# One level of Strassen–Winograd for both feed-forward products of a decoder layer

## The chip, the cores and the metric

The kernel runs on one core of one Trainium2 chip. The metric is device time in microseconds (us) of one execution. Five engines work side by side, each through its own queue of instructions in order: TensorE (PE in the profile, with its weight loads as PEld), VectorE (DVE), ScalarE (ACT), GpSimd (POOL) and SyncE (SP), which here issues the DMAs. SBUF is the on-chip memory, PSUM holds the matmul results, DRAM is the memory beyond.

## What is computed

The reference is one layer of a hybrid decoder, then a final norm, for 1024 tokens, model width 1024 and a feed-forward width of 4096, all in float32:

```
u = RMSNorm(h);  z = u @ W_in
branches: sparse attention, a gated recurrence, cross attention into 256 memory tokens
h += W_o( sum_b sigmoid(gate_b(u)) * y_b )
h += W_down( relu(RMSNorm(h) @ W_up)^2 )      # W_up 1024 x 4096, W_down 4096 x 1024
out = RMSNorm(h)
```

Only the last two lines and W_o bear on this change.

## The kernel before

Every float32 product is done in three passes (`mm3`, L219): each operand is split into a high part (`hi`, rounded to the fast type fp32r) and the rest (`lo`), and hi·hi, hi·lo and lo·hi are added up in PSUM. `split` makes the two: the high part is a copy on ACT (L216), the low part a subtraction (L217) on DVE or, if the caller says so, on POOL. A scheduler orders the instructions of each engine after the program has been written, so the source shows what depends on what, and a listing of the built program shows the order.

W_o (`out_proj`, L1002 to L1036) goes by eight tiles of 128 tokens: load `yr`, split it, 48 matmuls, add the residual (L1021), normalise (`rms_scale`, L203), transpose eight blocks on PE (L84), and write the normalised activations, scaled by `gmlp`, as `vh` and `vl` with the feature in the partition (L1033, L1034).

The feed-forward part (L1066 to L1119) goes by 16 blocks of two chunks of 128 of the 4096 hidden features. For a chunk and a half of the tokens, 24 matmuls give 128 x 512 of the hidden layer in the PSUM tile `psg`; ACT takes relu (L1083) and its square (L1084, the high part), DVE the square in float32 (L1085) and the low part (L1086). Then, for eight token tiles and two halves of the width, 12 matmuls give the block's share of the down product in `pss` or `pst`, and DVE adds it to `h`, which stays in SBUF (L1107). The next block's weights are loaded meanwhile (`uraw` 512 KB, `draw` 256 KB, SP's queue) and split by ACT and POOL. After the last block each token tile is normalised (L1109 to L1118) and written out (L1119).

Of the kernel before, what the change touches and what calls it, by code (L numbers as in the profile page):

```python
# [9 lines left out]
F32 = mybir.dt.float32  # L10
# [56 lines left out]
class TensorQueue:  # L67
    """TensorE's instructions, with the sum of their cost."""
# [7 lines left out]
    def matmul(self, out, w, x, start, stop):  # L76
        n = 1
        for d in out.shape[1:]:
            n *= d
        self.tc.nc.tensor.matmul(out, w, x, start=start, stop=stop)  # L80
        self._add(n)
# [54 lines left out]
def body(tc, A, out):  # L136
# [4 lines left out]
    with ExitStack() as top:  # L141
# [3 lines left out]
        w4 = top.enter_context(tc.tile_pool(name="w4", bufs=1))  # L145
# [32 lines left out]
        tn_d = dram.tile([KC, P, S], F32, name="tn_d")  # L178
        y_d = [dram.tile([KC, P, 512], F32, name=f"y_d{x}") for x in range(2)]
# [39 lines left out]
        def mm3(ps, sh, sl, mh, ml, first, last):  # L219
            pe.matmul(ps, sh, mh, start=first, stop=False)  # L220
            pe.matmul(ps, sh, ml, start=False, stop=False)
            pe.matmul(ps, sl, mh, start=False, stop=last)
# [12 lines left out]
        with ExitStack() as mid:  # L235

# [68 lines left out]
            with tc.tile_pool(name="e0", bufs=1) as e0:  # L305
# [32 lines left out]
                def load_const(name, shape):  # L338
                    t = const.tile(shape, F32, name="c_" + name)
                    dma(t, A[name])  # L340
                    return t

                gmlp = load_const("g_mlp", [P, KC])
# [7 lines left out]
                wmask = const.tile([P, 640], BF16, name="wmask")  # L351
# [6 lines left out]
                gates = const.tile([P, NQ, 48], F32, name="gates")  # L358
                cp = const.tile([P, KC], F32, name="cp")
                cn = const.tile([P, KC], F32, name="cn")  # L360
                cn2 = const.tile([P, KC], F32, name="cn2")
                KCAB = const.tile([P, G, 2, 64], F32R, name="KCAB")
                VC = const.tile([64, G, P], F32R, name="VC")
# [630 lines left out]
            vp = mid.enter_context(tc.tile_pool(name="vp", bufs=1))  # L994

            def v_tiles(name):
                return [[vp.tile([P, 4, 512], F32R, name=f"{name}{a}{b}") for b in range(2)] for a in range(2)]

            h = []
            vh = v_tiles("vh")  # L1000
            vl = v_tiles("vl")

            def out_proj():
                for j in range(NQ):
                    ts = slice(j * P, (j + 1) * P)
                    yh = w4.tile([P, KC, P], F32R, name="yh", tag="whi", bufs=2)
                    yl = w4.tile([P, KC, P], F32R, name="yl", tag="wlo", bufs=2)
                    for x in range(2):
                        yr = half2("yr").rearrange("p (c t) -> p c t", t=P)
                        dma(yr, y_d[j // 4][4 * x:4 * x + 4, :, (j % 4) * P:(j % 4) * P + P].rearrange("c p t -> p c t"))  # L1010
                        split(yh[:, 4 * x:4 * x + 4, :], yl[:, 4 * x:4 * x + 4, :], yr)
                    xt = st("xres")
                    dma(xt, A["x"][ts, :])
                    h.append(rw("h") if j < 6 else w4.tile([P, D], F32, name="h", tag="wraw", bufs=2))
                    for nh in range(2):
                        cs = slice(nh * 512, nh * 512 + 512)
                        ps = ps_g()
                        for k in range(KC):
                            woh, wol = wo[2 * nh + k // 4]
                            mm3(ps, yh[:, k, :], yl[:, k, :], woh[:, k % 4, :], wol[:, k % 4, :], k == 0, k == KC - 1)  # L1020
                        dve.scalar_tensor_tensor(h[j][:, cs], ps, 0.5, xt[:, cs], OP.mult, OP.add)  # L1021
                    r = rms_scale(h[j], xt)
                    dve.tensor_scalar(xt, h[j], r, None, OP.mult)
                    dst = tok_dst(vh, vl, j)
                    for kh in range(2):
                        pt = ps_s()
                        for k in range(4):
                            c = (kh * 4 + k) * P
                            pe.transpose(pt[:, k * P:(k + 1) * P], xt[:, c:c + P], ident)
                        dh, dl = dst(kh)  # L1030
                        for k in range(4):
                            g = gmlp[:, kh * 4 + k:kh * 4 + k + 1]
                            act.activation(dh[:, k, :], pt[:, k * P:(k + 1) * P], AF.Copy, scale=g)  # L1033
                            dve.scalar_tensor_tensor(dl[:, k, :], pt[:, k * P:(k + 1) * P], g, dh[:, k, :],  # L1034
                                                     OP.mult, OP.subtract)
                    yield  # L1036

            for _ in out_proj():
                pass

            def pair(name):
                t = big.tile([P, 2, S], F32R, name=name, tag="ut", bufs=8)
                return t[:, 0, :], t[:, 1, :]

            acts = [pair("act") for _ in range(4)]
            wds = [pair("wd") for _ in range(4)]
            NB = 2
            NBLK = FF // P // NB

            def load_up(fc):  # L1050
                raw = st("uraw", F32, (P, KC, P))
                dma(raw, A["w_up"][fc])
                wh = w4.tile([P, KC, P], F32R, name="uh2", tag="whi", bufs=2)
                wl = w4.tile([P, KC, P], F32R, name="ul2", tag="wlo", bufs=2)
                split(wh, wl, raw, lo_eng=pool)
                return wh, wl

            def load_down(fc):
                d_h, d_l = wds[fc % 4]
                for x in range(2):  # L1060
                    cs = slice(x * 512, x * 512 + 512)
                    raw = half2("draw")
                    dma(raw, A["w_down"][fc * P:(fc + 1) * P, cs])
                    split(d_h[:, cs], d_l[:, cs], raw, lo_eng=pool)

            up = [load_up(f) for f in range(NB)]  # L1066
            for f in range(NB):
                load_down(f)
            for fb in range(NBLK):
                fcs = [fb * NB + f for f in range(NB)]  # L1070
                order = [(f, hf) for f in range(NB) for hf in range(2)]
                if fb == 0:
                    order = [(f, hf) for hf in range(2) for f in range(NB)]
# [158 lines left out]
```

## Time and profile before

| what | value |
|---|---|
| runs | 2231.94 us median of 3 (2228.72 to 2233.19) |
| the profiled execution, first to last instruction | 2226.8 us |
| mean granted TensorE clock in it (1 is full speed) | 0.980 |
| PE busy | 94% of the span |
| DVE, ACT, POOL busy | 60%, 48%, 24% of the span |
| DMA | 191.20 MB |
| first feed-forward matmul issued, last one | 1511, 2217 us |

The page names each group of instructions by source line, engine and tiles (out<-in). The span is that of one profiled execution; the runs are timed from outside and lie about 5 us above it.

### The profile page before, as it was taken

Reading aid. Unit: us, or ns where it says so; the run is one execution under the profiler, and the core shown is the slowest. Engines: PE = TensorE matmul, PEld = TensorE weight load, DVE = VectorE, ACT = ScalarE, POOL = GpSimd, SP = SyncE. Lnnn points to the kernel's source line nnn. Section 1 sums busy time; section 2 is a strip of 40 time slices with the busy share of each in tenths; the row PEclk is TensorE's granted clock in tenths of the full one; section 3 lists DMA queues with packets and bytes.
Section 4 is the critical chain, followed back from the end, with each engine's and each line's share of the span. In section 5 each row is a group of like instructions: output and inputs, shape, how many; then the busy total and the mean of one; then the engine's idle time right before and its main releaser. Section 6 shows DMA issues by size and latency. Waiting matters only on the chain. (4 is left out here: it accounts for less than half of the span.)

```text
span 2226.8 us, 29553 instructions
## 1 busy us (share of the span) xinstructions
PE 2087.0 (94%) x10660; PEld 1740.7 (78%) x10660; DVE 1346.7 (60%) x3039; ACT 1064.4 (48%) x2073; POOL 545.5 (24%) x457
## 2 busy tenths in 40 slices
PE   6988989999999989989998998999999999999998
PEld 5867867887877877778777777787888888888886
DVE  6254386777687776878767768544344434444445
ACT  5244367677567665757666657543222122122213
POOL 2010011343323341234232333203222222122210
PEclk9999999999999999999999999999999999999999
DMA  5555345312331123231132342422111111111102
GB/s 183 155 178 171 109 114 149 100 57 58 95 100 49 41 73 123 63 120 47 41 93 77 109 142 76 149 76 95 53 52 48 38 57 48 48 48 57 48 20 76
DMA packets 112155, 191.20 MB, mean 86 GB/s; under 512 B 14216, under 2 KB 57992, under 8 KB 112008
## 3 DMA queue, kind: packets, MB, share of 16 engines
q1 hardware_dynamic: 112008, 189.30, 27.3%
q8 instruction: 84, 1.38, 0.3%
q14 instruction: 63, 0.52, 0.1%
HBM read 142.08 MB, written 47.19 MB: 85 GB/s over the span
## 5 line engine op out<-in xcount | busy, mean ns | idle before, releaser
L80 PE MATMUL psg<-uh,whi 128*128 128x512 f32 x928 | 384.0, 414 | 14.4 <-DVE qxl L217 7.7
L80 PE MATMUL psg<-uh,wlo 128*128 128x512 f32 x928 | 372.2, 401 | 0.5 <-DVE wlo L217 0.5
L80 PE MATMUL psg<-ul,whi 128*128 128x512 f32 x928 | 372.4, 401 | 0.0
L588 DVE TENSOR_TENSOR pw<-pst,ph 128x512 fp32r<-128x512 f32 (+1 forms) x352 | 217.9, 623 | 61.8 <-ACT ph L587 60.2
L587 ACT ACTIVATE ph<-pst 128x512 fp32r<-128x512 f32 (+1 forms) x352 | 187.9, 540 | 103.6 <-PE pst L84 96.7
L80 PEld LDWEIGHTS psg<-uh,whi 128*128 128x128 f32 x928 | 178.3, 192 | 42.3 <-DVE qxl L217 7.9
L80 PEld LDWEIGHTS psg<-uh,wlo 128*128 128x128 f32 x928 | 178.5, 192 | 39.6 <-issue 1.1
L1085 DVE TENSOR_TENSOR relu<-relu 128x512 f32<-128x512 f32 x64 | 79.3, 1239 | 209.0 <-ACT act L1084 209.0
L80 PE MATMUL psg<-vh,ul 128*128 128x512 f32 x512 | 200.0, 391 | 0.7 <-POOL ul L217 0.7
L80 PE MATMUL psg<-vh,uh 128*128 128x512 f32 x512 | 200.3, 391 | 0.0
L80 PE MATMUL psg<-vl,uh 128*128 128x512 f32 x512 | 200.0, 391 | 0.0
L80 PEld LDWEIGHTS psg<-ul,whi 128*128 128x128 f32 x928 | 179.2, 193 | 25.2 <-issue 0.7
L217 POOL TENSOR_TENSOR wlo<-wraw,whi 128x1024 fp32r<-128x1024 f32 (+1 forms) x58 | 127.6, 2201 | 285.3 <-ACT whi L216 270.7
L80 PE MATMUL pss<-wd,act 128*128 128x512 f32 x768 | 195.2, 389 | 0.0
L80 PE MATMUL pst<-wd,act 128*128 128x512 f32 x768 | 195.2, 389 | 0.0
L216 ACT ACTIVATE wd<-draw 128x512 fp32r<-128x512 f32 x64 | 40.2, 632 | 315.5 <-PE pss L80 248.2
L217 POOL TENSOR_TENSOR wd<-draw,wd 128x512 fp32r<-128x512 f32 x64 | 83.6, 1307 | 374.1 <-ACT wd L216 373.2
L80 PEld LDWEIGHTS pst<-wd,act 128*128 128x128 f32 x768 | 144.2, 188 | 30.3
L80 PEld LDWEIGHTS pss<-wd,act 128*128 128x128 f32 x768 | 144.2, 188 | 30.2
L1107 DVE TENSOR_TENSOR h<-h,pss 128x512 f32<-128x512 f32 x128 | 87.8, 686 | 115.9 <-PE pss L80 115.9
L80 PE MATMUL pss<-KA,Q 128*128 128x320 f32 (+5 forms) x416 | 145.1, 351 | 11.3 <-DVE sx L765 6.1
L80 PE MATMUL pss<-KB,Q 128*128 128x320 f32 (+5 forms) x416 | 135.9, 330 | 2.2 <-DMA KB<-q_lo 2.2
(290 smaller groups left out, 4414.1 us busy)
## 6 DMA issues: line engine op xcount, KB each, us to landing
wraw<-in_wz SPq DMA_DIRECT2D x59, 512.0 KB
draw<-in_w_down SPq DMA_DIRECT2D x64, 256.0 KB
uraw<-in_w_up SPq DMA_DIRECT2D x32, 512.0 KB
xn<-in_x SPq DMA_DIRECT2D x8, 512.0 KB
v_d<-vs SPq DMA_DIRECT2D x32, 128.0 KB
V<-v_d SPq DMA_DIRECT2D x8, 512.0 KB
KA<-q_hi SPq DMA_DIRECT2D x16, 256.0 KB
KB<-q_lo SPq DMA_DIRECT2D x16, 256.0 KB
```

Of the source, the lines that this page charges most:

```text
L80: self.tc.nc.tensor.matmul(out, w, x, start=start, stop=stop)
L216: act.activation(hi, src, AF.Copy)
L217: (lo_eng or dve).tensor_tensor(lo, src, hi, OP.subtract)
L587: act.activation(ph[:rows, :w], pt[:rows, :w], AF.Copy)
L588: dve.tensor_tensor(pw[:rows, :w], pt[:rows, :w], ph[:rows, :w], OP.subtract)
L1085: dve.tensor_tensor(r, r, r, OP.mult)
L1107: dve.tensor_tensor(h[j][:, cs], h[j][:, cs], ps, OP.add)
```

## The change

Both feed-forward products are cut into 2 x 2 blocks and done by Winograd's form of Strassen's scheme: seven block products in place of eight, with sums of blocks made before and after. The products come in the order 1, 6, 2, 5, 7, 3, 4 (`ORDER_P`).

The up product: blocks of 512 features by 512 tokens; a step `(p, s)` is product s of the pair of chunks p and p+16, that is 12 matmuls of 128 x 512; the seven of a pair make 84, where 96 stood. `out_forms` and the `split`s behind it make the token-side operands: three blocks (`B11`, `B21`, `B22`) and four sums (`T1` to `T4`). `prep` makes the weight sums `su` on POOL and splits them into `uf`, `LEAD` = 6 products ahead. `run` multiplies, `finish` evicts (a chain of adds on DVE), squares, and makes the sums `as1` to `as4` of the squared activations on POOL that the down product wants; all seven go to the DRAM scratch `act_d` (256 KB each, 7 x 16 of them).

The down product: for each s, a loop over the 16 p with 12 matmuls each, into four PSUM banks that stay open. `fetch` reads `araw` back from `act_d`; w_down comes once and stays in SBUF (`wd`, `wdf`, `wdu`: 64 loads of 256 KB), and POOL makes its sums from the resident tiles (L1267, L1271, L1275 with its second add, L1282). `operands` splits both sides into `df`. At p = 15 of each s the banks are evicted; `h` comes back from the DRAM scratch `h_d`. Half of the token tiles are normalised and written out after s = 3, the other half after s = 4.

W_o is written so that the transposes of tile j come after the matmuls of tile j+1, the gain `g_mlp` is multiplied in as a broadcast tile `gmb`, and the pools of the earlier stages (`mc`, `w4`) are closed before it.

```diff
+            w4_stack.close()
...
+            def prep(p, s):
...
+                def tmp(n, x, y, op):
+                    sums[p, n] = tmp_tile("su")
+                    pool.tensor_tensor(sums[p, n], x, y, op)
+
+                if s == 6:
+                    tmp(5, a21, a22, OP.add)
+                    tmp(6, sums[p, 5], a11, OP.subtract)
+                elif s == 7:
+                    tmp(7, a11, a21, OP.subtract)
+                elif s == 3:
+                    tmp(3, a12, sums[p, 6], OP.subtract)
...
+                split(t[:, 0, :], t[:, 1, :], src, lo_eng=pool if s in (2, 5) else dve)
+
+            def product(ps, p, s, first):
+                t = forms.pop((p, s))
+                bh, bl = B[FORM_B[s]]
+                for k in range(4):
+                    ks = slice(k * P, (k + 1) * P)
+                    mm3(ps, t[:, 0, ks], t[:, 1, ks], bh[:, k, :], bl[:, k, :], first and k == 0, k == 3, not first)
...
+                def square(n, c, eng):
+                    acts[p, n] = act_tile("sq")
+                    if eng is pool:
+                        pool.tensor_tensor(acts[p, n], c, c, OP.mult)
+                    else:
+                        dve.scalar_tensor_tensor(acts[p, n], c, 0.0, c, OP.max, OP.mult)
...
+                elif s == 2:
+                    r = ev_tile("r11")
                     act.activation(r, ps, AF.Relu)
...
+                    square("11", r, pool)
+                elif s == 5:
+                    ev[p, "v"] = ev_tile("v")
+                    dve.tensor_tensor(ev[p, "v"], ps, ev[p, "u2"], OP.add)
...
+                    pool.tensor_tensor(s1, a21, a22, OP.add)
+                    pool.tensor_tensor(s2, s1, a11, OP.subtract)
+                    pool.tensor_tensor(s3, a11, a21, OP.subtract)
+                    acts[p, "s2"] = s2
+                    for i, t in ((1, a11), (4, a22), (5, s1), (6, s2), (7, s3)):
+                        dma(act_d[i - 1][p], t)
...
+            run(0, 1)
+            finish(0, 1)
+            out_forms(NQ - 1, prev)
+            run(0, 2)
+            for n, src in (("t2", "22"), ("t1", "12"), ("t3", "11"), ("t4", "21")):
+                B[n] = vform("T" + n[1], False)
+                for k in range(4):
+                    split(B[n][0][:, k, :], B[n][1][:, k, :], vr[src][:, k, :], lo_eng=pool if k % 2 else dve)
+            ox_stack.close()
+
+            ux = mid.enter_context(tc.tile_pool(name="ux", bufs=1))
...
+            def tmp_tile(name):
+                return ux.tile([P, 512], F32, name=name, tag="s", bufs=4)
...
+            def operands(s, p, araw):
+                t = form("df")
+                split(t[:, 0, :], t[:, 1, :], araw)
+                w = wd[p][0]
+                eng = dve
+                if s == 1:
+                    pool.tensor_tensor(w[1], w[1], w[0], OP.subtract)
+                    src = w[0]
+                elif s == 6:
+                    src = tmp_tile("dt2")
+                    pool.tensor_tensor(src, w[3], w[1], OP.subtract)
+                elif s == 4:
+                    src = tmp_tile("dt4")
+                    pool.tensor_tensor(src, w[1], w[3], OP.subtract)
+                    pool.tensor_tensor(src, src, w[2], OP.add)
                 else:
...
+                    src = {2: w[2], 5: w[1], 7: w[0], 3: w[3]}[s]
+                    eng = pool
+                b = form("df")
+                split(b[:, 0, :], b[:, 1, :], src, lo_eng=eng)
+                if s == 6:
+                    pool.tensor_tensor(w[0], src, w[0], OP.subtract)
+                return t, b
...
+                for j in range(4):
+                    js = slice(j * P, (j + 1) * P)
+                    mm3(banks[name][j], a[:, 0, js], a[:, 1, js], b[:, 0, :], b[:, 1, :], fresh_bank and p == 0, p == NP - 1,
+                        not fresh_bank)
...
+                        o = [tmp_tile("o") for _ in range(2)]
```

The order that results, at three places. POOL before, between the last weights of W_o (`wol`) and the first ones of the feed-forward part (`wd`, `ul2`):

```order
L217 TENSOR_TENSOR wol_14710<-woraw_14707,woh_14709 128x1024
L217 TENSOR_TENSOR wol_14710<-woraw_14713,woh_14709 128x1024
L217 TENSOR_TENSOR wd_15517<-draw_15533,wd_15517 128x512
L217 TENSOR_TENSOR wd_15517<-draw_15537,wd_15517 128x512
L217 TENSOR_TENSOR wd_15518<-draw_15541,wd_15518 128x512
L217 TENSOR_TENSOR ul2_15524<-uraw_15521,uh2_15523 128x1024
L217 TENSOR_TENSOR wd_15518<-draw_15545,wd_15518 128x512
```

POOL after, from the last token tile of W_o on: `vr11`, `vr21` and `vr22` are sums of activation blocks in float32, `T1l` to `T4l` their low parts, `su` the weight sums of the first p.

```order
L1065 TENSOR_TENSOR vr21_14736<-vr21_14736,vr22_14738 128x4x128
L1066 TENSOR_TENSOR vr11_14735<-vr22_14738,vr11_14735 128x4x128
L220 TENSOR_TENSOR T2l_15491<-vr22_14738,T2h_15490 128x512 x2
L220 TENSOR_TENSOR T1l_15501<-vr12_14737,T1h_15500 128x512 x2
L220 TENSOR_TENSOR T3l_15511<-vr11_14735,T3h_15510 128x512 x2
L220 TENSOR_TENSOR T4l_15521<-vr21_14736,T4h_15520 128x512 x2
L1088 TENSOR_TENSOR su_15538<-urb_14742 128x512
L1088 TENSOR_TENSOR su_15540<-su_15538,ura_14741 128x512
L1127 TENSOR_TENSOR sq_15536<-r11_15534 128x512
L1088 TENSOR_TENSOR su_15552<-ura_14741,urb_14742 128x512
L1088 TENSOR_TENSOR su_15557<-ura_14741,su_15540 128x512
L220 TENSOR_TENSOR uf_15549<-su_15538,uf_15549 128x512
```

Six weight splits of POOL stood here, which the matmuls need one after the other; now ten subtractions for the token side stand ahead of the two `su` (L1088) from which the form of product (0, 6) is split.

POOL before, in the middle of the feed-forward part, one block's weights:

```order
L217 TENSOR_TENSOR ul2_16506<-uraw_16503,uh2_16505 128x1024 [waits DMAHW4_49,PE_49,Activation_49]
L217 TENSOR_TENSOR wd_15519<-draw_16785,wd_15519 128x512 [waits DMAHW7_49,Activation_49]
L217 TENSOR_TENSOR wd_15519<-draw_16789,wd_15519 128x512 [waits DMAHW0_49,Activation_49]
L217 TENSOR_TENSOR wd_15520<-draw_16793,wd_15520 128x512 [waits DMAHW3_49,Activation_49]
L217 TENSOR_TENSOR wd_15520<-draw_16797,wd_15520 128x512 [waits DMAHW4_49,Activation_49]
L217 TENSOR_TENSOR ul2_16776<-uraw_16773,uh2_16775 128x1024 [waits DMAHW1_49,PE_49,Activation_49]
```

POOL after, in the down product at s = 6: `dt2` is a sum of two w_down tiles, `wdu` the resident w_down tile that the next sums want.

```order
L1271 TENSOR_TENSOR dt2_18715<-wdu_18271 128x512 [waits DMAHW2_49,DVE_49,Pool_49]
L1282 TENSOR_TENSOR wdu_18271<-dt2_18715,wdu_18271 128x512 [waits Pool_49]
L1271 TENSOR_TENSOR dt2_18739<-wdu_18295 128x512 [waits DMAHW3_49,DVE_49,Pool_49]
L1282 TENSOR_TENSOR wdu_18295<-dt2_18739,wdu_18295 128x512 [waits Pool_49]
L1271 TENSOR_TENSOR dt2_18763<-wdu_18319 128x512 [waits DMAHW4_49,DVE_49,Pool_49]
L1282 TENSOR_TENSOR wdu_18319<-dt2_18763,wdu_18319 128x512 [waits Pool_49]
```

Before, one block (48 matmuls times four) had six of POOL's instructions; now each step of 12 matmuls has two.

DVE before, near the end, where token tiles are normalised and written out (`o`):

```order
L1107 TENSOR_TENSOR h<-h,pst 128x512 [waits PE_49]
L1115 RECIPROCAL rms_r<-rms_r 128x1 [waits Activation_49]
L1118 SCALAR_TENSOR_TENSOR o<-h,rms_r,gf 128x512 [waits DVE_49]
L1118 SCALAR_TENSOR_TENSOR o<-h,rms_r,gf 128x512
L1112 TENSOR_SCALAR rms_r<-rms_s_19872 128x1 [waits Activation_49]
L1107 TENSOR_TENSOR h<-h,pss 128x512 [waits PE_49]
L1113 TENSOR_SCALAR rms_r<-rms_r 128x1 [waits DVE_49]
L1107 TENSOR_TENSOR h<-h,pst 128x512 [waits PE_49]
L1107 TENSOR_TENSOR h<-h,pss 128x512 [waits PE_49]
```

DVE after, at the passage from s = 3 to s = 4 in the down product: `o` again, `hh` the other half of a token's row, `du_18836` and `du_18841` the half just finished, `dt_20277` the weight sum of step (4, 1):

```order
L1353 TENSOR_SCALAR rms_r<-rms_r 128x1 [waits DVE_49]
L1355 RECIPROCAL rms_r<-rms_r 128x1 [waits Activation_49]
L1358 SCALAR_TENSOR_TENSOR o<-hh,rms_r,gf 128x512 [waits DMAHW5_49,DVE_49]
L1358 SCALAR_TENSOR_TENSOR o<-du_18836,rms_r,gf 128x512 [waits DMAHW7_49]
L1352 TENSOR_SCALAR rms_r<-rms_s_20258 128x1 [waits Activation_49]
L1353 TENSOR_SCALAR rms_r<-rms_r 128x1 [waits DVE_49]
L1355 RECIPROCAL rms_r<-rms_r 128x1 [waits Activation_49]
L1358 SCALAR_TENSOR_TENSOR o<-hh,rms_r,gf 128x512 [waits DMAHW6_49,DMAHW0_49,DVE_49]
L1358 SCALAR_TENSOR_TENSOR o<-du_18841,rms_r,gf 128x512 [waits DMAHW1_49]
L220 TENSOR_TENSOR df<-dt_20277,df 128x512 [waits Activation_49]
L220 TENSOR_TENSOR df<-araw,df 128x512 [waits DMAHW3_49,Activation_49]
```

Before, only the adds of finished PSUM tiles stood between the `o`; now the split of step (4, 1), on which PE's next matmuls wait, stands behind the last `o` of s = 3.

## Rows read from the trace of the kernel before

**Rows 1.** The page's first part: span, and busy time of the engines.

```profile
span 2226.8 us, 29553 instructions
PE 2087.0 (94%) x10660; PEld 1740.7 (78%) x10660; DVE 1346.7 (60%) x3039; ACT 1064.4 (48%) x2073; POOL 545.5 (24%) x457
```

**Rows 2.** Windows: us, busy us of each engine, granted clock, DMA share, GB/s.

```profile
core 0: us, PE busy (x) PEld busy (x) DVE busy (x) ACT busy (x) POOL busy (x), PEclk, DMA share, GB/s
0.00:20.00 20.00, 6.25 (x24) 4.43 (x24) 11.86 (x24) 12.94 (x25) 7.04 (x11) 1.00 0.91 352
1411.00:1511.00 100.00, 96.48 (x443) 77.50 (x442) 50.02 (x111) 44.93 (x101) 13.58 (x8) 1.00 0.32 101
1511.00:1526.00 15.00, 10.87 (x39) 8.45 (x38) 5.83 (x11) 5.57 (x14) 4.92 (x3) 0.77 0.36 123
1600.00:1700.00 100.00, 100.00 (x443) 82.71 (x442) 41.11 (x54) 21.78 (x33) 24.60 (x16) 1.00 0.14 49
2100.00:2200.00 100.00, 100.00 (x442) 82.68 (x441) 42.17 (x58) 19.20 (x32) 12.80 (x8) 1.00 0.06 22
```

**Rows 3.** DVE's groups, 1526 to 2200 us: busy us, mean ns, idle before.

```profile
L1107 DVE TENSOR_TENSOR h<-h,pss 128x512 f32<-128x512 f32 x122 | 83.7, 686 | 115.9 <-PE pss L80 115.9
L1085 DVE TENSOR_TENSOR relu<-relu 128x512 f32<-128x512 f32 x64 | 79.3, 1239 | 209.0 <-ACT act L1084 209.0
L1086 DVE TENSOR_TENSOR act<-relu,act 128x512 fp32r<-128x512 f32 x64 | 46.1, 720 | 1.6
```

**Rows 4.** ACT's groups in the same stretch.

```profile
L216 ACT ACTIVATE wd<-draw 128x512 fp32r<-128x512 f32 x60 | 37.8, 632 | 314.0 <-PE pss L80 248.2 <-DMA draw<-in_w_down 55.6 <-PE pst L80 10.2
L1083 ACT ACTIVATE relu<-psg 128x512 f32<-128x512 f32 x63 | 37.1, 590 | 97.0 <-PE psg L80 97.0
```

**Rows 5.** Timeline of POOL: start us, duration us.

```profile
1538.31 2.41 POOL L217 TENSOR_TENSOR ul<-uraw,uh 128x1024 fp32r<-128x1024 f32 x1
1540.67 1.75 POOL L217 TENSOR_TENSOR wd<-draw,wd 128x512 fp32r<-128x512 f32 x1
1542.45 2.78 POOL L217 TENSOR_TENSOR ul<-uraw,uh 128x1024 fp32r<-128x1024 f32 x1
1561.96 2.65 POOL L217 TENSOR_TENSOR wd<-draw,wd 128x512 fp32r<-128x512 f32 x2 [16.73 <-ACT wd L216]
```

**Rows 6.** Timeline of DVE at the same time.

```profile
1539.49 1.78 DVE L1085 TENSOR_TENSOR relu<-relu 128x512 f32<-128x512 f32 x1 [5.18 <-ACT act L1084]
1541.30 1.67 DVE L1086 TENSOR_TENSOR act<-relu,act 128x512 fp32r<-128x512 f32 x1
1543.55 2.23 DVE L1085 TENSOR_TENSOR relu<-relu 128x512 f32<-128x512 f32 x1
```

**Rows 7.** Timeline of all engines where W_o ends.

```profile
1510.88 0.39 PE L80 MATMUL psg<-woh,yl 128*128 128x512 f32 x1
1515.70 1.06 ACT L216 ACTIVATE uh<-uraw 128x1024 fp32r<-128x1024 f32 x1 [2.52 <-DMA uraw<-in_w_up]
1516.66 0.19 ACT L208 ACTIVATE rms_r<-rms_r 128x1 f32<-128x1 f32 x1
1516.83 2.34 POOL L217 TENSOR_TENSOR ul<-uraw,uh 128x1024 fp32r<-128x1024 f32 x1 [3.25 <-ACT uh L216]
1517.08 2.64 DVE L1023 TENSOR_SCALAR xres<-h,rms_r 128x1024 f32<-128x1024 f32 x1
1519.78 1.97 PE L84 MATMUL pss<-ident,xres 128*128 128x128 f32 x8 [3.47 <-DVE xres L1023]
```

**Rows 8.** Timeline of the end.

```profile
2217.03 0.68 DVE L1107 TENSOR_TENSOR h<-h,pst 128x512 f32<-128x512 f32 x1
2217.07 0.63 ACT L1109 ACTIVATE o<-h 128x512 f32<-128x512 f32 x1 [0.56 <-DVE rms_r L1113]
2221.09 1.42 DVE L1118 SCALAR_TENSOR_TENSOR o<-h,rms_r,gf 128x512 f32<-128x512 f32 x2
```

**Rows 9.** The chain of waits at the end: start us, us, what.

```profile
2219.06 2.04 DMA out<-o
```

More of the change, by code (lines that the diff above doesn't have):

```diff
@@ L74, in _add, with matmul @@
         self.cost += cols / 2400.0 + 0.0025
-    def matmul(self, out, w, x, start, stop):
+    def matmul(self, out, w, x, start, stop, more=False):
         n = 1
@@ L79, in matmul @@
             n *= d
-        self.tc.nc.tensor.matmul(out, w, x, start=start, stop=stop)
+        self.tc.nc.tensor.matmul(out, w, x, start=start, stop=stop, skip_group_check=more)
         self._add(n)
@@ L217, in split, with mm3 @@
             (lo_eng or dve).tensor_tensor(lo, src, hi, OP.subtract)
[L219 to L222, printed above, removed]
+        def mm3(ps, sh, sl, mh, ml, first, last, more=False):
+            pe.matmul(ps, sh, mh, start=first, stop=False, more=more)
+            pe.matmul(ps, sh, ml, start=False, stop=False, more=more)
+            pe.matmul(ps, sl, mh, start=False, stop=last, more=more)
         lo_engine = [dve]
@@ L992, in body @@
             ap_stack.close()
[L994 to L1056, printed above, removed]
@@ L1058, in load_down @@
[L1058 to L1077 removed]
+            mc_stack.close()
@@ new lines, in body, with load_up, flat @@
+            NP = FF // P // 2
+            ORDER_P = (1, 6, 2, 5, 7, 3, 4)
+            FORM_B = {1: "11", 2: "21", 3: "22", 4: "t4", 5: "t1", 6: "t2", 7: "t3"}
+            raws, sums, forms = {}, {}, {}
+            def load_up(p):
+                if p < NP and p not in raws:
+                    raws[p] = [wraw("ura"), wraw("urb")]
+                    for t, f in zip(raws[p], (p, p + NP)):
+                        dma(t, A["w_up"][f])
+            def flat(t):
+                return t.rearrange("p k n -> p (k n)")
@@ new lines, in body @@
+            steps = [(0, 1), (0, 2), (0, 6), (0, 5), (0, 7), (0, 3), (0, 4)]
+            steps += [(p, s) for p in range(1, NP) for s in ORDER_P]
+            prev = None
+            load_up(0)
+            for j in range(NQ):
+                xt = out_tile(j)
+                if prev is not None:
+                    out_forms(j - 1, prev)
+                prev = xt
+                if j in (3, 5):
+                    prep(0, 1 if j == 3 else 2)
+            run(0, 1)
+            finish(0, 1)
@@ new lines, in act_tile @@
+            def act_tile(name):
+                return ux.tile([P, 512], F32, name=name, tag="a", bufs=11)
+            LEAD = 6
+            finish(0, 2)
+            todo = steps[2:]
+            at = 0
+            for n, (p, s) in enumerate(todo):
+                while at < len(todo) and at <= n + LEAD:
+                    q, u = todo[at]
+                    load_up(q)
+                    prep(q, u)
+                    at += 1
+                    load_up(q + 1)
+                run(p, s)
+                finish(p, s)
@@ new lines, in need, with fetch @@
+            def need(p, c):
+                load_down(p)
+                t, got = wd[p]
+                if c not in got:
+                    got.add(c)
+                    f = p + NP * (c // 2)
+                    dma(t[c], A["w_down"][f * P:(f + 1) * P, (c % 2) * 512:(c % 2) * 512 + 512])
+                return t[c]
+            def fetch(s, p):
+                araw = tmp_tile("araw")
+                dma(araw, act_d[s - 1][p])
+                for c in {1: (0, 1), 6: (3,), 2: (2,)}.get(s, ()):
+                    need(p, c)
+                return araw
```

243 lines of the change are left out of this document (198 added, 45 removed).

## The prediction

> **What bounds the kernel now.** I read the page's first part first: PE is busy for 2087.0 of 2226.8 us, so only fewer matmuls, or less waiting, can shorten the kernel by much [rows 1]. The windows then say where it is bound: from 1600 to 2200 us PE is busy for all of each 100 us at granted clock 1.00, while DVE is busy for some 41, ACT 19 to 22 and POOL 13 to 25 of 100 [rows 2]. In that stage one matmul of 128 x 512 takes 100 / 442 = 0.2262 us. The 3072 feed-forward matmuls should take 695 us; they lie between 1510.9 us, where W_o's last one starts [rows 7], and 2217 us, where DVE takes up the last result [rows 8], which is 706. So the stage loses 11 us, most of it between 1511 and 1526 us, where PE is busy for 10.87 of 15 at clock 0.77 [rows 2]. This is the passage from W_o: the transposes of the last token tile wait 3.47 us for their input [rows 7].
>
> DVE's and POOL's groups come next, because the change gives these engines work. DVE's add from PSUM takes 686 ns, the low part 720, and the square, of the same size, 1239 [rows 3]. The two timelines show why. POOL's subtractions and DVE's operations with two SBUF inputs never finish side by side here: POOL ends at 1540.72 us, DVE (start 1539.49, 1.78 long) at 1541.27, POOL at 1542.42, DVE at 1542.97, POOL at 1545.23, DVE at 1545.78 [rows 5, 6]. From end to end a DVE operation costs 0.55 and POOL's 128 x 512 one 1.15 us; two of POOL's in a row, with nothing between, take 2.65, or 1.33 each [rows 5]. I shall count the two engines' operations of this kind as one queue, the **shared lane**.
>
> **The change, part by part.**
>
> *Matmuls.* Two products of 16 x 7 x 12 = 1344 matmuls stand for two of 1536: 384 fewer, at 0.2262 us, **-86.9 us**. A step of 12 takes 2.71 us, a p of the up product (84) 19.0. Each matmul keeps a weight load of its own, which lies beside PE's work now too (82.7 of 100 us) [rows 2].
>
> *Up product.* For each p POOL has 11 operations (four `su`, the low parts of s = 2 and 5, one square, four sums), DVE eight with two SBUF inputs (five low parts, three squares) and five adds from PSUM, ACT seven high parts at 0.63 and two copies at 0.59 [rows 4], 5.6 us. In the shared lane: eight pairs at 1.15 + 0.55 and three more POOL operations at 1.33 make 17.6 us, against PE's 19.0. By full durations it would be 11 x 1.33 + 8 x 0.72 = 20.4, or 22 us more over 16 p. POOL's operations that wait for PE (the square, `as1`) have the `LEAD` of six products, about 16 us, behind them. I take +3 us (0 to +22), for the lane is nearest to the alternating rows.
>
> *Start of the feed-forward part.* After the last transposes POOL has ten subtractions and two `su` ahead of the form of product (0, 6), which PE needs third: two at 1.33 and, where DVE's eight low parts alternate with its own, 1.15 + 0.55. That is 8 x 1.70 + 4 x 1.33 = 18.9 us, and 1.4 for the split of the form (ACT 0.63, DVE 0.72). Product (0, 2), 2.7 us, lies beside it; product (0, 1) stands before the transposes and hides part of their wait. PE is idle for some 17.6 us, then waits about 3 for the low part of s = 5, which is four places further in POOL's queue, and runs at the lower clock for a while, as it did in the window at 1511. Some 23 us are lost where 11 were: **+12** (+8 to +18). Late next is what POOL has to catch up.
>
> *Down product.* A step of 2.71 us costs the lane: s = 1, one POOL and two DVE operations, 2.25; s = 2, 5, 7 and 3, one low part on each engine, 1.70; s = 6 and s = 4, two and two, 3.40. So s = 6 and s = 4 are bound by the lane: +0.69 a step. Sixteen steps make +11; the eight `df` tiles hold up to three steps of lead at the start of s = 6, which leaves 13 x 3.40 - 43.4, about +1, if the lead is full. I take **+5** for s = 6 (0 to +20, where the upper end has full durations, 4.10 a step).
>
> *From s = 3 to s = 4.* This wait is new. The split of step (4, 1) stands on DVE's queue behind all eight `o`. From the last matmul of s = 3: an add 0.69, two squares on ACT at 0.63, two `o` 1.42 [rows 3, 8], and read-outs, a square root and small operations, which I put at 1.0, so 4.4 us for the first tile. Each further one costs 1.9, and the third must wait until the first one's `o` are written out, since `o`, `araw` and `dt4` share four tiles: 2.04 [rows 9]. Sum 4.4 + 3 x 1.9 + 2 = 12 us, of which step (4, 0) covers 2.7. PE waits about 9.5 (5 to 14) and then starts s = 4 without a lead, 14 steps at +0.69: another 9.5 (0 to 20). **+19** for s = 4.
>
> *End.* After the last matmul four tiles stand to be normalised in place of one, with four `o` tiles: the same 4.4 + 3 x 1.9 + 2 = 12 us and the last write, 2.04, against 2226.8 - 2217.0 = 9.8: **+4** (+1 to +6). DMA writes of the first tiles lie beside it.
>
> *DMA.* The up product writes 7 x 256 KB and reads 1 MB for each p: 2.9 MB in 19 us, 151 GB/s. The down product reads 112 + 64 times 256 KB, of which 96 fall into s = 1 and s = 6 (87 us): 290 GB/s. The highest row is 352 GB/s at a DMA share of 0.91 [rows 2]. On SP's queue the loads of `ura` and `urb` for later p stand among the writes of earlier squares and sums and wait for these; the `LEAD` gives them more than a p of 19 us. I count it as hidden, with **+5** for the passages between stages (first loads of s = 1, `h` and its adds on POOL at the ends of s = 6 and s = 5; 0 to +15).
>
> *W_o.* The transposes no longer wait for the same tile, but 1.5 MB (`gmb`, `ura`, `urb`) are asked for ahead of `yr`, and closing the pools makes the first tiles wait for the earlier stages. PE was busy 96.48 of 100 us there [rows 2], so 3.5 at most can be won; 1.5 MB at 352 GB/s are 4.5 us if nothing hides them. **+1** (-3 to +8).
>
> The sum: -86.9 + 3 + 12 + 5 + 19 + 4 + 5 + 1 = -38. The span becomes 2189 us; the median of the runs lies 5.1 above the profiled span (2231.94 to 2226.8), so **2194 us**. All low ends together give -76 or 2156, all high ends +36 or 2268.
>
> The Trainium skill ("SBUF — State Buffer", "SBUF: two separate sides") calls the pair of ports that DVE and GpSimd share "an exclusive lock, not a bandwidth split", held for the whole instruction. The trace agrees that one waits for the other to end, but the price from end to end is 0.55 and 1.15 us, less than the 0.72 and 1.33 of the operations alone [rows 3, 5, 6]. Held for all of the latter, the sum would be the one of the second rival, below.
>
> **The rivals.**
>
> *Ceiling.* The lane hides all through (leads suffice) and the passage at s = 4 costs only its wait. -86.9 + 0 + 10 + 0 + 9.5 + 3 + 0 + 0 = -64: **2167 us**. For it: 17.6 is below 19.0. Against it: 3.40 is above 2.71.
>
> *Full durations.* As in the rule, POOL's and DVE's operations do not overlap at all: +22 in the up product, s = 6 and s = 4 at 4.10 a step, +10 and +10 more than I took: -38 + 19 + 10 + 10 = +1 against before: **2233 us**, no change. Against it: six ends in a row that say 1.70 a pair [rows 5, 6].
>
> *DMA.* The 96 loads of s = 1 and s = 6, 25 MB, move at 248 GB/s or so in place of 352 because DRAM is written and read in small pieces of a queue that SP serves in order: 101 us for 87: +14, **2208 us**. For it: `araw` and `dt2` share four tiles, so only two `araw` are on their way. Against it: 352 at the start of this kernel.
>
> *Slower: POOL's queue in the up product.* POOL stands still at the square of s = 2 and at `as1` until PE and DVE have delivered, and the subtractions behind it, on which PE waits next, are late: each engine waits for the other once a p. ACT shows such a thing now: a high part that waits for its DMA holds up the square root behind it until 1516.66 us, and with it the transposes [rows 7]. The other terms sum to +46, so it decides where a p takes 19.0 + (86.9 - 46) / 16 = 21.6 us, that is 4 us of standing still on top of the lane's 17.6; at 22.5 us the time is **2246 us**. Against it: the lead of six products.
>
> **How the numbers follow.** My forecast has a chance of 0.49, with its own range 2172 to 2215 (the start and s = 4 at either of their ends); ceiling 0.15; DMA 0.10; full durations 0.08, spread as 0.03 faster, 0.02 same and 0.03 slower; slower by POOL's queue 0.13. That start, lane and s = 4 together eat the gain to within 0.2%, about what a measurement of this kernel can tell from no change, is another 0.05. Faster is 0.49 + 0.15 + 0.10 + 0.03 = 0.77, same 0.07, slower 0.16. The range of 8 in 10 reaches from the ceiling, 2160, to where the time is plainly slower, 2238.
>
> **What would show it.** Right: 84 up matmuls in 19 to 19.5 us; PE idle for 15 to 20 us after W_o; s = 6 near 48 and s = 4 near 62 us against 43.4; DVE's squares and POOL's sums stretched to 1.8 and 1.75 us. Wrong: a p of 21 us or more with PE waiting for `uf` (POOL is the bound), PE waiting for DMA in s = 1 or s = 6, or a granted clock below 1.00 through whole stages, since every wait then costs twice.

## The result

The changed kernel takes 2259.68 us (median; 2254.28 to 2261.33) where the one before takes 2230.33 (2226.87 to 2233.19) beside it: a ratio of 1.0124, 95% interval 1.0105 to 1.0142. It is slower by 1.2%, where 2194 us and a chance of 0.77 for faster were forecast. The page of the profiled execution answers to [rows 1]:

```profile
span 2256.4 us, 30093 instructions
PE 2022.8 (90%) x10276; PEld 1677.6 (74%) x10276; DVE 1407.0 (62%) x3011; ACT 1128.6 (50%) x2193; POOL 881.8 (39%) x709
```

PE has 64 us less work than before and the span is 29.6 us longer, so some 94 us of PE standing still were added. The matmuls left out are worth 86.9 us, so those that are left took some 23 us longer; that goes with the granted clock, 0.962 on the mean where it was 0.980. Five windows of the changed kernel (us, busy us of each engine, granted clock, DMA share, GB/s) answer to [rows 2]: the start of W_o, the wait before product (0, 6), the up product, s = 4, and the first 5 us after one of PE's waits in s = 4.

```profile
core 0: us, PE busy (x) PEld busy (x) DVE busy (x) ACT busy (x) POOL busy (x), PEclk, DMA share, GB/s
1418.00:1435.30 17.30, 0.00 (x0) 0.00 (x0) 7.90 (x4) 2.93 (x4) 8.39 (x4) 0.60 0.49 160
1537.70:1557.20 19.50, 0.00 (x0) 0.00 (x0) 13.08 (x10) 9.69 (x19) 19.10 (x13) 0.58 0.11 42
1600.00:1700.00 100.00, 100.00 (x443) 82.84 (x442) 55.51 (x68) 28.15 (x48) 82.84 (x59) 1.00 0.44 156
2172.00:2243.00 71.00, 53.57 (x180) 41.07 (x180) 27.85 (x33) 18.30 (x34) 39.54 (x28) 0.78 0.14 41
2211.00:2216.00 5.00, 5.00 (x12) 3.94 (x13) 1.82 (x4) 1.15 (x2) 3.21 (x3) 0.50 0.36 105
```

In the up product PE is as full as before, though POOL is now busy for 83 of 100 us. The loss lies elsewhere, and PE's waits (engine, tile and line, what it waited for: us in total, times, longest) name it:

```profile
engine line waited for: us in total, times, longest us
PE psg L80 <- ACT df L219: 37.3, 7, 19.1
PE pst L80 <- ACT uf L219: 19.5, 1, 19.5
PE psg L80 <- DMA urb<-in_w_up: 17.3, 1, 17.3
PE pss L80 <- DVE df L220: 7.1, 11, 0.7
PE psg L80 <- POOL df L220: 6.7, 3, 2.8
```

The 17.3 us stand before W_o's first matmul. The profile puts them down to `urb`, but that matmul reads `yh`, the split of `yr`, which ends just ahead of it (timeline below).

From PE's timeline, the times of the first and last matmul of each stage give the whole account against before (before: the end of W_o at 1511.1, the end of PE's last matmul at 2216.7):

| stretch | after | at 0.2262 us a matmul | loss against the rate | against before | forecast |
|---|---|---|---|---|---|
| matmuls left out | | | | -86.9 | -86.9 |
| to the end of W_o | ends 1529.3 | | | +18.2 | +1 |
| from there to the first down matmul, 1862.8 | 333.5 | 304.0 | 29.5 | +18.8 (10.7 were lost before) | +15 |
| down product, to 2242.4 | 379.6 | 304.0 | 75.6 | +75.6 | +29 |
| from there to the end, 2256.4 | 14.0 | | | +3.9 | +4 |

The sum is +29.6. Two entries are far off: the end of W_o by 17 us, the down product by 47. The +18.2 at W_o are three parts: the wait of 17.3, PE's work ahead of it, which ended 6.6 us later than before (1418.0 in place of 1411.4), and W_o itself, which takes 94.0 us in place of 99.7. The seven stages of the down product, 43.5 us each at PE's rate, from the first matmul of each to that of the next:

| kernel | s = 1 | 6 | 2 | 5 | 7 | 3 | 4 |
|---|---|---|---|---|---|---|---|
| after | 44.7 | 54.3 | 46.7 | 43.5 | 51.1 | 47.6 | 91.7 |
| e1_dt_own | 48.3 | 49.5 | 46.6 | 43.5 | 58.4 | 47.6 | 65.9 |
| e2_all_dve | 43.5 | 43.5 | 43.5 | 43.5 | 47.1 | 47.6 | 66.6 |
| e3_o_in_place | 44.5 | 54.7 | 48.2 | 43.5 | 51.1 | 47.6 | 75.5 |
| e6_forms | 45.0 | 49.9 | 48.1 | 43.5 | 49.7 | 43.5 | 75.5 |
| e9_tiles | 50.9 | 48.4 | 47.8 | 43.5 | 55.5 | 43.5 | 54.3 |
| e7_combo | 44.0 | 43.5 | 43.5 | 43.5 | 47.3 | 47.6 | 49.6 |
| e8_early | 43.9 | 43.5 | 43.5 | 43.5 | 43.8 | 43.5 | 46.1 |

The other rows are the experiments below. Three timelines of the changed kernel (start us, duration us) show the places. First POOL and DVE at s = 6, one step and the start of the next:

```profile
1937.16 1.62 POOL L1271 TENSOR_TENSOR dt<-wdu 128x512 f32<-128x512 f32 x1 [0.68 <-POOL wdu L1282]
1938.85 1.30 POOL L1282 TENSOR_TENSOR wdu<-dt,wdu 128x512 f32<-128x512 f32 x1
1939.47 1.23 DVE L220 TENSOR_TENSOR df<-dt,df 128x512 fp32r<-128x512 f32 x1 [1.85 <-ACT df L219]
1940.62 0.68 DVE L220 TENSOR_TENSOR df<-araw,df 128x512 fp32r<-128x512 f32 x1
1940.83 1.62 POOL L1271 TENSOR_TENSOR dt<-wdu 128x512 f32<-128x512 f32 x1 [0.68 <-POOL wdu L1282]
```

From end to end: the sum `dt` ends at 1938.78, `wdu` at 1940.15, DVE's two low parts at 1940.70 and 1941.30, the next sum at 1942.45. The four follow one another without a gap, 3.67 us a step, and the new sum waits 0.68 us for DVE's low part of the old one (the profile names POOL's own `wdu`, which had ended at 1940.15). Next, the passage from s = 3 to s = 4:

```profile
2152.11 0.75 DVE L1358 SCALAR_TENSOR_TENSOR o<-hh,rms_r,gf 128x512 f32<-128x512 f32 x1
...
2158.01 5.55 SPq L1359 DMA_DIRECT2D out<-o  x4
...
2160.07 0.63 ACT L1350 ACTIVATE o<-du 128x512 f32<-128x512 f32 x1 [3.07 <-DMA out<-o]
...
2164.64 0.63 ACT L1350 ACTIVATE o<-du 128x512 f32<-128x512 f32 x1 [3.08 <-DMA out<-o]
...
2169.27 1.26 POOL L1274 TENSOR_TENSOR dt<-wd 128x512 f32<-128x512 f32 x1 [23.12 <-DMA out<-o]
...
2172.59 3.23 PE L80 MATMUL psg<-df 128*128 128x512 f32 x6 [19.06 <-ACT df L219]
```

POOL's sum of step (4, 1) stands still for 23.12 us and is released by the write of an `o` to DRAM, not by DVE: it gets a tile only when the fourth token tile has left. The token tiles themselves wait in the same way: ACT's second square of the third and of the fourth starts only when an `o` has been written, after waits of 3.07 and 3.08 us, so each of these comes some 4.5 us after the one ahead. Then s = 4 itself, on PE:

```profile
2193.78 2.93 PE L80 MATMUL psg<-df 128*128 128x512 f32 x6 [6.14 <-ACT df L219]
2204.80 1.52 PE L80 MATMUL psg<-df 128*128 128x512 f32 x6
2210.93 2.93 PE L80 MATMUL psg<-df 128*128 128x512 f32 x6 [3.25 <-ACT df L219]
2231.46 2.93 PE L80 MATMUL psg<-df 128*128 128x512 f32 x6 [6.69 <-ACT df L219]
```

PE waits 6.14, 3.25 and 6.69 us, at every fourth step. After each such wait six matmuls take 2.93 us in place of 1.52: the granted clock is 0.50 there, the lower of its two levels (1.2 GHz), and 0.78 on the mean of the stage (windows above).

### The profile page after: what moved, and what is told of

Same layout as the page of the kernel before. It is cut to its first block, busy times and chain, and to the rows that moved or that the text cites. A ratio compares the mean times of both kernels' runs of the same rounds, so it can differ in the third digit from the quotient of the medians.

```text
span 2256.4 us, 30093 instructions
## 1 busy us (share of the span) xinstructions
PE 2022.8 (90%) x10276; PEld 1677.6 (74%) x10276; DVE 1407.0 (62%) x3011; ACT 1128.6 (50%) x2193; POOL 881.8 (39%) x709
## 3 DMA queue, kind: packets, MB, share of 16 engines
q8 instruction: 81, 1.33, 0.3%
## 5 line engine op out<-in xcount | busy, mean ns | idle before, releaser
L220 DVE TENSOR_TENSOR df<-araw,df 128x512 fp32r<-128x512 f32 x112 | 99.4, 899 | 120.8 <-ACT df L219 119.5
L80 PE MATMUL psg<-df 128*128 128x512 f32 x384 | 106.9, 413 | 44.7 <-ACT df L219 37.3
L80 PE MATMUL pso<-ph,V 128*128 128x256 f32 (+1 forms) x544 | 129.7, 304 | 3.9 <-DVE fold L599 3.6
L773 ACT ACTIVATE E<-E,sx 128x128 f32<-128x128 f32 (+7 forms) x128 | 98.7, 772 | 57.9 <-DVE sx L769 57.4
L80 PEld LDWEIGHTS psg<-df 128*128 128x128 f32 x384 | 75.2, 200 | 66.9 <-ACT df L219 40.3
L80 PE MATMUL pso<-pw,V 128*128 128x256 f32 (+1 forms) x544 | 122.6, 291 | 1.3 <-DVE pw L592 1.3
L219 ACT ACTIVATE whi<-wraw 128x1024 fp32r<-128x1024 f32 (+2 forms) x83 | 82.8, 997 | 76.6 <-PE psg L80 51.1
L773 ACT ACTIVATE Ew<-Ew,sx 128x640 f32<-128x640 f32 (+4 forms) x128 | 88.4, 691 | 64.6 <-DVE sx L769 64.4
L80 PE MATMUL pss<-df 128*128 128x512 f32 x432 | 109.8, 394 | 10.0 <-DVE df L220 7.1
L80 PEld LDWEIGHTS pso<-ph,V 128*128 128x128 f32 x544 | 95.1, 190 | 21.7 <-issue 7.0
```

The lines of the kernel that those rows point to most:

```text
L80: self.tc.nc.tensor.matmul(out, w, x, start=start, stop=stop, skip_group_check=more)
L219: act.activation(hi, src, AF.Copy)
L220: (lo_eng or dve).tensor_tensor(lo, src, hi, OP.subtract)
L773: act.activation(E[:, :nw], E[:, :nw], AF.Exp, bias=sx[:, hh:hh + 1], scale=-1.0, accum_out=sx[:, 2 + hh:3 + hh])
```

## The experiments

All but the last three kernels were timed once (beside 2230.91 or, for e5 and e6, a median of 2231.78 us of the kernel before); the changed kernel's own times lie 7 us apart, so the stages of these kernels are compared, not totals of a few us.

**Own tiles for the weight sums.** `araw`, `dt2`, `dt4` and `o` share four tiles. Here the two sums take tiles of a tag with seven, of which three are free:

```diff
-                    src = tmp_tile("dt2")
+                    src = piece("dt2")
...
-                    src = tmp_tile("dt4")
+                    src = piece("dt4")
```

> The weight sums dt2 and dt4 of the down product take tiles of another tag (seven, three of them free) in place of one of the four that araw, dt and o share. Shared-lane theory (DVE's two-input operations and POOL's run one after the other): s = 6 stays at 3.4 to 3.7 us a step, 52 to 54 us in all, and the whole kernel within some 8 us of the changed one. Tile theory (one free tile for dt makes sum, split and update a chain): s = 6 falls to about 45 us and s = 4 from 92 to about 65, the kernel to about 2225 us.

2232.4 us. Both were half right. s = 4 falls from 91.7 to 65.9, as the tile theory has it, and the gap of 19.1 us after s = 3 to waits of 0.7 and 2.5. s = 6 falls only to 49.5, and the timeline of POOL and DVE shows a lane that is full, but in a better order:

```profile
1927.71 1.62 POOL L1282 TENSOR_TENSOR wdu<-dt,wdu 128x512 f32<-128x512 f32 x1
1928.10 1.78 DVE L220 TENSOR_TENSOR df<-araw,df 128x512 fp32r<-128x512 f32 x1
1929.29 1.74 POOL L1271 TENSOR_TENSOR dt<-wdu 128x512 f32<-128x512 f32 x1
1929.80 1.77 DVE L220 TENSOR_TENSOR df<-dt,df 128x512 fp32r<-128x512 f32 x1
1931.11 1.62 POOL L1282 TENSOR_TENSOR wdu<-dt,wdu 128x512 f32<-128x512 f32 x1
```

POOL's operations and DVE's now alternate, each 1.6 to 1.8 us long from start to end, but from the end of the other engine's to its own end POOL's take 1.15 and DVE's 0.55, and a step takes 1931.11 - 1927.71 = 3.40 us. That is the price of the prediction, 2 x 1.15 + 2 x 0.55, to the hundredth.

**All on DVE.** Every operation that the feed-forward part has on POOL goes to DVE:

```diff
-                    pool.tensor_tensor(sums[p, n], x, y, op)
+                    dve.tensor_tensor(sums[p, n], x, y, op)
...
-                    eng = pool
+                    eng = dve
```

> All of the feed-forward part's operations on POOL go to DVE, nothing else changes. Shared-lane theory: a POOL operation holds the lane for 1.15 to 1.33 us and the same one on DVE for 0.60, so s = 6 falls from 3.68 to 2.7 us a step (44 us in all), the wait of 19.5 us before product (0, 6) falls to about 10, the up product stays at 19.0 us a p (DVE then has 24 operations, some 15 us, a p), the kernel falls by 25 to 35 us, to about 2228. Tile theory: s = 6 stays above 50 us, since there is still one tile for dt. If DVE's own queue is the limit: the up product rises above 20 us a p.

2201.4 us, better than expected. s = 6 runs at PE's rate; DVE's timeline has the same four operations in 2.65 us:

```profile
1909.82 0.69 DVE L1271 TENSOR_TENSOR dt<-wdu 128x512 f32<-128x512 f32 x1
1910.54 0.69 DVE L1282 TENSOR_TENSOR wdu<-dt,wdu 128x512 f32<-128x512 f32 x1
1911.15 0.69 DVE L220 TENSOR_TENSOR df<-araw,df 128x512 fp32r<-128x512 f32 x1
1911.75 0.69 DVE L220 TENSOR_TENSOR df<-dt,df 128x512 fp32r<-128x512 f32 x1
1912.47 0.69 DVE L1271 TENSOR_TENSOR dt<-wdu 128x512 f32<-128x512 f32 x1
```

With its work doubled, DVE is faster than two engines that take turns: each operation starts some 0.6 to 0.73 us after the one ahead. The wait before product (0, 6) fell from 19.5 to 13.8 (10 were expected), and from (0, 6) to the down product 301.1 us pass in place of 305.6. The tile theory alone, which left s = 6 above 50, is out. The wait after s = 3 stays: 17.7 us.

**`o` in place.** The normalised row is written over its source, and the unused output of the squares goes to the PSUM bank just read:

```diff
-                        o = [tmp_tile("o") for _ in range(2)]
...
-                            act.activation(o[x], halves[x], AF.Square, accum_out=ss[:, x:x + 1])
+                            act.activation(ps, halves[x], AF.Square, accum_out=ss[:, x:x + 1])
...
-                            dma(out[tok * P:(tok + 1) * P, xs], o[x])
+                            dma(out[tok * P:(tok + 1) * P, xs], halves[x])
```

> The normalised rows are written over the halves that they come from, and the squares' unused output goes to the PSUM bank just read, so o needs none of the four shared tiles. If the tiles (o waits for its DMA, dt4 for o) make the wait of 19.1 us after s = 3, it falls to about 5 us and the kernel by about 14, at the end some 2 more. If DVE's queue makes it (the split of step (4, 1) behind the eight o), about 9 us stay.

2236.33 us; s = 4 falls by 16.2, and PE's longest wait at the passage is 3.3 us:

```profile
2153.84 1.20 PE L80 MATMUL psg<-df 128*128 128x512 f32 x4 [3.31 <-ACT df L219]
```

So the tiles made the gap, as own tiles for the sums show from the other side (0.7 and 2.5 us), and DVE's queue costs a few us at most.

**The start of W_o**, in two kernels. One asks for `gmb` after the first token tile's loads and, as shown, for `ura` and `urb` after the second's:

```diff
...
-            load_up(0)
             for j in range(NQ):
                 xt = out_tile(j)
+                if j == 1:
+                    load_up(0)
```

> The loads of gmb and of the first w_up chunks (ura, urb) are asked for after the first token tile's own loads. If they hold up yr on the queue, the wait of 17.3 us before W_o falls to about 12 and the kernel by about 5. If it is only that the new tiles lie over memory of the stage before, whose last readers end at 1427.7 us, it stays at about 16.

The other takes W_o's last low parts off POOL:

```diff
-                    split(wo[-1][0][:, xs, :], wo[-1][1][:, xs, :], raw, lo_eng=pool)
+                    split(wo[-1][0][:, xs, :], wo[-1][1][:, xs, :], raw, lo_eng=(pool, dve)[nh])
```

> The changed kernel with one edit: the last four low parts of W_o's weights (wol, 128 x 1024) go from POOL to DVE. Before W_o starts, DVE's last two merges of the stage ahead (gm, L990 and L991) take 1.75 to 2.82 us each beside these, in place of 0.69, and the new tiles wait for them. If the lane holds up the start of W_o through them, the wait before W_o's first matmul falls from 14 to 17 us to about 10 and the end of W_o comes 5 us earlier; if it is the loads on the queue, nothing moves.

2255.17 and 2256.19 us, both within the changed kernel's own range, so the waits decide: 17.3 us falls to 14.1 and to 12.2, where the five experiments that leave this part alone have 16.8 to 17.1. The changed kernel's timeline shows both causes:

```profile
1416.20 10.19 POOL L220 TENSOR_TENSOR wol<-woraw,woh 128x1024 fp32r<-128x1024 f32 x4 [15.30 <-ACT woh L219]
1421.48 2.71 DVE L991 TENSOR_TENSOR gm<-gm,ymerge 128x512 f32<-128x512 f32 x1
1424.11 2.82 DVE L990 SCALAR_TENSOR_TENSOR gm<-gm,ymerge 128x512 f32<-128x512 f32 x1
...
1428.57 0.45 SPq L1029 DMA_DIRECT2D yr<-y_d  x1
1430.16 0.43 SPq L1077 DMA_DIRECT2D urb<-in_w_up  x1
1430.63 0.43 SPq L1029 DMA_DIRECT2D yr<-y_d  x1
1434.64 0.63 ACT L219 ACTIVATE yh<-yr 128x512 fp32r<-128x512 f32 x1 [14.35 <-DMA yr<-y_d]
1435.33 0.79 PE L80 MATMUL psg<-woh,yh 128*128 128x512 f32 x1 [17.33 <-DMA urb<-in_w_up]
```

DVE's merges `gm` take 2.7 and 2.8 us beside four of POOL's 128 x 1024 subtractions, and SP asks for `yr` only after the last of them; then 1 MB of weights stands between the two halves of `yr`, and the split of the first comes 6.1 us after it was asked for. With both edits, in the run of five edits, the wait is 9.0: 5.2 until `yr` is asked for, 3.1 until its split starts, 0.7 for the split. Why `yr` is asked for so late was not tried: it could wait for its place in SP's queue, behind the last merges' writes, or for memory that the closed pools still had in use. The ends of W_o vary by 4 us among kernels that share this part, since PE's work ahead of it ends between 1413.5 and 1418.0, so they decide nothing; how much of the 6.6 us of the account is of this kind stays open.

**Form tiles.** In the down product both operands of a step go round eight `form` tiles in two pools. Here the activations take the five of one and the weights the three of the other:

```diff
-                t = form("df")
+                t = ux.tile([P, 2, 512], F32R, name="df", tag="form", bufs=5)
...
-                b = form("df")
+                b = fx.tile([P, 2, 512], F32R, name="df", tag="form", bufs=3)
...
```

> The changed kernel with one edit: in the down product the activations' splits take the five form tiles of one pool and the weights' splits the three of the other, in place of both going round both pools. If the order in which the form tiles come free is what puts every fourth activation split behind later ones on ACT (0.72 us of PE every fourth step in s = 7 and s = 3, and the waits of 3 to 7 us every fourth step in s = 4), s = 3 falls from 47.6 to 43.5 us and s = 4 by some 10 to 15; if these come from the four shared tiles alone, s = 4 keeps its 92 us.

2230.99 us, some 29 us less from a choice of tiles. s = 3 reaches PE's rate, s = 4 gets 16 us shorter. In the changed program's order on ACT, each fourth activation split stands behind weight sums that come later (`df_20366` belongs to the step of `df_20372`):

```
L219 ACTIVATE df_20372<-dt4_20369 128x512
L219 ACTIVATE df_20389<-araw_20341 128x512
L219 ACTIVATE df_20395<-dt4_20392 128x512
L219 ACTIVATE df_20412<-araw_20364 128x512
L219 ACTIVATE df_20366<-araw_20318 128x512
```

So PE waits at each fourth step for a later step's split. This is the period of four in s = 4 and the 0.72 us in s = 7 and s = 3. In s = 4 the later step's sum is late as well, because it waits on the lane and on its tile: with the lane gone (all on DVE) these waits are 0.7 to 0.8 us there, with own tiles 0.7 to 1.1, with waits of up to 3.2 for DVE's low parts behind them.

s = 6 falls too, to 49.9 with steps of 3.40 us, though `dt` kept the four shared tiles. In the built changed program all sixteen `dt` of s = 6 lie at one address; in this one they go round all four. So the one tile did make the chain of 3.67 us a step; that the four shared ones came down to one was a choice of the scheduler's, and own tiles for `dt` or form tiles of their own both undo it.

**The three tile edits alone** (own tiles, `o` in place, form tiles), POOL as it was:

> The changed kernel with the three edits on tiles alone (own tiles for dt, o in place, form tiles), POOL keeps all its work. What is left in the down product should be the shared lane: a step of s = 6 and of s = 4 at 3.40 us, two POOL and two DVE operations in turn, less the lead: 46 to 52 us for s = 6, 50 to 56 for s = 4, 43.5 to 45 for the other five. With the start of W_o (17 us) and the wait before product (0, 6) (19.5 us) as they were, 2200 to 2215 us, faster than before by 1%. If the lane is not the limit, s = 6 and s = 4 come to 44 to 47 us and the time to about 2195.

2219.99 us, 0.9955 of before (0.9938 to 0.9972), five us above what was expected: s = 4 and s = 6 came as expected, but s = 1 and s = 7 grew to 50.9 and 55.5, as they had with own tiles alone (48.3 and 58.4). The timeline shows how, in s = 7:

```profile
2060.91 1.26 POOL L1274 TENSOR_TENSOR dt<-wd 128x512 f32<-128x512 f32 x1
...
2066.25 1.26 POOL L220 TENSOR_TENSOR df<-wdf,df 128x512 fp32r<-128x512 f32 x1
2067.56 2.50 PE L80 MATMUL psg<-df 128*128 128x512 f32 x5 [6.47 <-POOL df L220]
```

Since `dt` has tiles to spare, POOL makes sums of s = 4 (L1274, L1275) ahead of the low parts of s = 7, and PE waits 6.47 us for one of these. At s = 1 it is the sum and update of s = 6 (L1271, L1282, from 1870.73 us on) that stand ahead of the last `as4`: its write to `act_d` is asked for 16.9 us after the first down matmul, where it was 14.0, and the loads of s = 1 stand behind it on SP's queue. No run here took these sums back; with all on DVE too the two stages do not grow. Near the end of s = 4 the steps lie 3.40 us apart, the lane's price again:

```profile
2192.71 1.43 PE L80 MATMUL psg<-df 128*128 128x512 f32 x5 [0.38 <-DVE df L220]
2196.11 1.43 PE L80 MATMUL psg<-df 128*128 128x512 f32 x5 [0.39 <-DVE df L220]
```

**The five edits together** (all but the form tiles):

> The five edits together (all on DVE, own tiles for dt, o in place, late loads, W_o's low parts on DVE). Lane and tile theories together: s = 1, 6, 2, 5 at 43.5 us each, s = 4 at 47 to 52, the wait before product (0, 6) about 14, W_o's end some 8 us earlier: 2175 to 2185 us. If one of the two theories is wrong, s = 4 stays above 60 and the time above 2195.

2174.62 us, 0.9748 of before (0.9724 to 0.9772), at the low end of what was expected. PE's longest waits that are left:

```profile
PE pst L80 <- ACT uf L219: 13.8, 1, 13.8
PE psg L80 <- ACT yh L219: 9.0, 1, 9.0
```

**With the form tiles, and an early start.** The weight sums of p = 0 go to a form tile that is free while T1 to T4 are still made, so that two forms are ready:

```diff
+            su0 = iter([(t[:, x, :]) for t in [form("su0", F32)] for x in range(2)])
+
+            def tmp_tile(name):
+                return next(su0)
+
             run(0, 2)
+            prep(0, 6)
...
+                if n == "t2":
+                    prep(0, 5)
...
```

> The same, and the form tiles as in the run on forms, and the weight sums and forms of products (0, 6) and (0, 5) made from a tile that is free before the token sums T1 to T4 are done. If POOL's and DVE's queue of token sums was the wait before product (0, 6), it falls from about 14 to 5 us (then some 4 us before product (0, 7)); s = 7 and s = 3 at 43.5 us; 2160 to 2172 us.

2157.71 us, **0.9674 of before (0.9647 to 0.9701)**: the change beats the kernel before by 3.3% once the new work no longer waits for itself, 2 us below the expected range. Of the wait before (0, 6) 1.2 us are left, and 4.2 us before (0, 7), as expected:

```profile
PE psg L80 <- ACT yh L219: 9.1, 1, 9.1
PE pss L80 <- ACT uf L219: 4.2, 1, 4.2
PE psg L80 <- ACT df L219: 1.5, 2, 1.2
PE pst L80 <- ACT T2h L219: 1.2, 1, 1.2
```

## Why the prediction was wrong

The time came out 66 us above the forecast of 2194. Step by step:

- *Matmuls, -86.9*: right for the matmuls at full clock. PE keeps 443 in 100 us in the up product.
- *Up product, +3*, and *start, +12*: together 15 forecast, 18.8 measured. The up product is bound by PE: each p from the second on takes 19.04 us, 0.5 us in all above the rate, though POOL is busy for 83 of 100 us. The other 18 are the start, at the upper end of its range. PE's wait was 19.5 us where 17.6 were worked out, and there was no wait for the low part of s = 5 but one of 2.4 us before product (0, 3), for DVE. That the queue of token sums ahead of the `su` made the 19.5 is shown by POOL, busy for 19.10 of these 19.50 us, and by the early sums (1.2 are left); with the same queue all on DVE, busy for all but 0.07 us of it, the wait is 13.8.
- *Lane prices, 1.15 and 0.55*: right. Steps of 3.40 us appear in two experiments. "Full durations", 4.10 a step, did not occur. The Trainium skill ("SBUF — State Buffer", "SBUF: two separate sides") has one engine blocked for the other's whole instruction; the trace agrees in that nothing overlaps at the ends, and has the smaller price beside it.
- *s = 6, +5*: 10.8. The lane's price was right, but two things beside it were not. The one tile for `dt` made the order sum, update, low part, low part (3.67 a step) in place of taking turns, and the lead was about one step in place of three (54.3 / 3.67 = 14.8 steps; 49.5 / 3.40 = 14.6 with own tiles).
- *From s = 3 to s = 4, +19*: this is the step that failed. It cost 48. I had put the wait of 9.5 us on DVE's queue, behind the eight `o`, with one write of 2 us for the shared tiles. It was 19.1 us, and the tiles were its cause: with `o` out of them it fell to 3.3, with `dt` out of them to 0.7 and 2.5. I had counted 1.9 us for each further token tile and one write for all; the third and the fourth took 4.5 each, because each had to wait for a write, and so had the sum of step (4, 1). I also took 0.69 a step for the rest, the lane's price. The waits after the gap were 16.4 us in sum (0.32, 6.14, 3.25, 6.69), from the permuted order and from sums late by lane and tile, as all on DVE, own tiles and form tiles show. With the gap's 19.1 they make 35.5; the other 12.7 of the 48.2 are steps that themselves took longer. Some 10.6 of it are the four steps that follow the waits, at the clock of 0.50 (5.29 us in place of 2.72 after each of the last three), a term that I had only for the start. My sign of a clock below 1.00 came true in this one stage (0.78 on the mean), but a wait did not cost twice: 2.6 us came on top of 6.14, 3.25 and 6.69.
- *Passages, +5*: s = 1, 2, 7 and 3 lose 1.2, 3.2, 7.6 and 4.1, together 16. The 4.1 of s = 3 are the form tiles' order, which I had not seen, since they go with that edit; those of s = 2 go with all on DVE, and of those of s = 7 4.0 go with all on DVE and 3.5 more with the form tiles (47.3 to 43.8 between the last two kernels).
- *W_o, +1*: the second failure, +18. Two mechanisms were named (loads ahead of `yr`, closed pools) but bounded by 8, as if 1.5 MB were all; the third, POOL's hold on the merges, was not. Of the wait of 17.3 us 3 are shown for the loads and 5 for POOL's hold. The other 9 stay open between SP's queue and memory. W_o itself won 5.7 us, more than the 3.5 that I had as the most.
- *End, +4*: 3.9. With `o` in place it is 2.6 us shorter, so here the write of the shared tiles was counted rightly.

Of the rivals none is what happened. DMA was not the bound: s = 1 moved 322 GB/s and lost 1.2 us, s = 6 138. (The 96 loads that I gave these two stages are 80; sixteen loads of w_down belong to s = 2.) POOL's queue did not slow the up product. The side that I had given 0.16 came from a cause that I had seen as a detail: four tiles shared by three kinds of data with different lifetimes.

## What to carry to other kernels

Count for every shared tile tag who holds its tiles longest; a tile that is read by a DMA out makes the next sum wait for DRAM, and a listing of the program's order shows which split is put behind it. Before moving work to an idle engine, price it where both engines meet: a step that takes 3.40 us on POOL and DVE together took 2.65 on DVE alone. A scheme that saves matmuls is worth its saving only where every step's preparation fits under that step; e8_early turned +1.2% into -3.3% with the same 2688 matmuls.

## What was not expected of the hardware

Two engines can be slower than one of them: a subtraction of 128 x 512 costs 1.15 to 1.33 us on POOL and starts 0.60 to 0.73 us after the last on DVE, and the engines took turns so strictly that a pair lasted 1.70 us in the kernel before, in e1_dt_own and in e9_tiles alike. After PE's waits of 6.14, 3.25 and 6.69 us in s = 4 the next twelve matmuls ran at a granted clock of 0.50 (5.29 us for a step of 2.72); in s = 3, with its four waits of 0.72 us, the granted clock stayed at 1.00.
